# A feed-forward stage whose first two chunks are turned back by VectorE and transfers, with six up chunks first

## The chip, the cores and the metric

The kernel runs on one core of one Trainium2 chip. The metric is the device time of one execution in microseconds (us). In the profile's rows PE is TensorE (matrix products), PEld its weight loads, DVE is VectorE, ACT is ScalarE, POOL is GpSimd and SP is SyncE, whose queue issues most transfers.

## The reference

One decoder layer on a sequence of 256 positions and 1024 channels, in float32: a mixer of two branches (an mLSTM and block attention), a residual layer norm, then a gated MLP with a causal convolution and a second residual layer norm. The change touches only the MLP:

```python
def conv_gated_mlp(x, w_up, conv_ffn, w_down):
    u = causal_dwconv(jnp.einsum("bsd,df->bsf", x, w_up), conv_ffn)   # 3 taps over positions
    g, up = jnp.split(u, 2, axis=-1)                                  # 2816 channels each
    return jnp.einsum("bsf,fd->bsd", jax.nn.silu(g) * up, w_down)
# x = layer_norm(ALPHA * x + ffn, ln2_g, ln2_b)
```

## The kernel before

All weights are cut into chunks of 128 x 2048 numbers, which are worked off in one list (`chunk_order`, L45). One turn of the loop in `run` (L338) is one step: it puts out the elementwise work that the step before left behind, the splitting of the weights that are needed two steps later, the load of the chunk five steps ahead (`load`, three buffers), and then the step's matrix products. The order of the instructions on each engine is the order in which the program writes them; nothing is rearranged afterwards. Three buffers hold split weights and three banks (`ps_main`) hold results of chunks.

Every float32 product is made of three products of rounded parts. A tile is split by `split_into` (L92): ACT casts it to a high part, DVE subtracts that from the original and leaves the low part. `mm3` (L143) multiplies high by high, high by low and low by high.

The MLP has 22 up chunks and 11 down chunks. Up chunk i makes 128 gate channels and 128 value channels. `mm_feat` gives them with channels on partitions and positions along the free dimension: 16 accumulations of three matrix products, 48 in all. `up_evac` (L1095) then returns two pieces of elementwise work. `conv` scales by the last tap on ACT (L1107, two instructions) and adds the other two taps on DVE (L1111, four). `gate` applies Silu on ACT (L1118), multiplies on DVE (L1122), and splits the product into the hidden tile's high and low part `hh` (ACT, L94) and `hl` (DVE, L95); six buffers hold each. Down chunk d uses hidden tiles 2d and 2d + 1, first all products of the one, then all of the other, and accumulates into four banks (`step_dn`, L1131).

Up chunks 0 and 1 are different, because the first layer norm finishes the two halves of the positions one after the other. They are computed together with positions on partitions (`mm_tok`), first for the first 128 positions and then for the others. Their results have to be turned so that channels lie on partitions. In the kernel before, ACT copies the two results to `tu` (L1072), PE turns them by eight transposes of 128 x 128 between the two halves of up chunk 2 (`back`, L1074), and the elementwise work of chunks 0 and 1 is put out together with that of chunk 2, in the step of up chunk 3.

How elementwise work and weight splitting interleave is written out by hand: `elem_work` (L381) goes through a list in which `None` means "now one piece of the weights' splitting". `self.mixed[s]` may rewrite the list of step s. The attention part already turns tiles without PE: `turn` (L636) transposes 32 x 32 blocks on DVE and writes the result to memory in DRAM, and `turn_in` (L646) reads it back by four transfers in which the blocks have changed places; both transfers go through SP's queue.

Of the kernel before, what the change touches and what calls it, by code (L numbers as in the profile page):

```python
# [10 lines left out]
F32 = mybir.dt.float32  # L11
F32R = mybir.dt.float32r
# [6 lines left out]
P = 128  # L19
S = 256  # L20
# [4 lines left out]
NF = D_FF // P  # L25
# [19 lines left out]
def chunk_order():  # L45

    order = [("o", c) for c in range(4)]
    for g in range(NG):
        order += [("qm", g), ("qb", g), ("km", g), ("kb", g), ("vm", g), ("vb", g), ("ga", g), ("gb", g)]
    for c in (0, 2):  # L50
        order += [("wa", c), ("wa", c + 1), ("wb", c), ("wb", c + 1)]
    order += [("wo", c) for c in range(4)]
    order += [("up", i) for i in range(4)]
    for d in range(8):
        order += [("dn", d), ("up", 2 * d + 4), ("up", 2 * d + 5)]
    order += [("up", 20), ("up", 21), ("dn", 8), ("dn", 9), ("dn", 10)]
    assert sum(k == "up" for k, _ in order) == NF and sum(k == "dn" for k, _ in order) == NF // 2
    return order

# [13 lines left out]
class Kernel:  # L73
# [106 lines left out]
    def run(self):  # L180
# [4 lines left out]
        dram = ctx.enter_context(tc.tile_pool(name="dram", bufs=1, space=DRAM))  # L185
# [51 lines left out]
        for k, (s, c) in enumerate(cut):  # L237
            dma(xraw[:, k], self.xt_d[:, k])
            for t in (2, 3, s) if k < 2 else (2, s, 3):
                if t == s:  # L240
                    dma(raw[s][:, c], self.wst[s, :, c])
                elif k in pieces:
                    d = slice(k * 256, (k + pieces[k]) * 256)
# [13 lines left out]
        for k, (s, c) in enumerate(cut):  # L257
# [3 lines left out]
            n = pieces.get(k, 0)  # L261
            d = slice(k * 256, (k + n) * 256)
# [50 lines left out]
        for s, (kind, i) in enumerate(self.order):  # L313
            if kind == "qm":
# [3 lines left out]

        self.table = dram.tile([8, LTOE], F32, name="table")
        self.mrows = dram.tile([4, S], F32, name="mrows")  # L320
        self.flip = [[dram.tile([m, P, n * P], F32, name=f"flip{g}{i}")
                      for i, (m, n) in enumerate(((1, 3), (1, 3), (2, 2))[:3 if g < NG - 1 else 2])] for g in range(NG)]
        self.gates_schedule(bif)
# [14 lines left out]
        for s, (kind, i) in list(enumerate(self.order))[4:]:  # L338
# [25 lines left out]
            parts = [] if late else self.split_parts(s + 2)  # L364
# [268 lines left out]
        self.mixed[b + 2] = lambda w: w + [e1b, None, e1c, None, e1d, e1e]  # L633


    def turn(self, t, d):  # L636

        m, _, f = d.shape
        n, w = t.shape[1], t.shape[1] // m
        tmp = self.ap.tile([P, 4 * P], F32, tag="turn", name="turn", bufs=2)[:, 0:n * P]  # L640
        for k in range(m):
            self.nc.vector.transpose(tmp[:, k * f:(k + 1) * f].rearrange("p (b c i) -> p c b i", b=4, i=32),
                                     t[:, k * w:(k + 1) * w].rearrange("p c (b i) -> p c b i", b=4))
        self.nc.sync.dma_start(d.rearrange("m p f -> p m f"), tmp.rearrange("p (m f) -> p m f", m=m))
# [9 lines left out]
    def group_schedule(self, g):  # L654
# [212 lines left out]
        if g == 0:  # L867
            at(self.side_elem, 6, lambda: self.floor_exp())
        at(self.side_elem, 5 + o, turn(0))
        if last:  # L870
            self.mixed[b + 6] = lambda w: ([back(0), lambda: el_l(1), lambda: el_e(1), el_n1] + w
# [174 lines left out]
    def step_up(self, s, i, *a):  # L1046
        if i == 0:

            self.hid = {}
            self.pt_up = [self.ps_side([P, 2, S], f"ps_up{j}") for j in range(2)]  # L1050
        if i < 2:
            ks = list(range(i, KT)) + [0] * i
            for k in ks:
                if i == 0 and k == KT - 1:
                    self.x1_transpose(1, 0)
                for m in ((0, 1), (2,)) if (i, k) == (1, 1) else ((0, 1, 2),):
                    for j in range(2):
                        self.mm_tok(s - i + j, [self.pt_up[j][:, t, :] for t in range(2)], self.x1h, self.x1l,
                                    toks=(i,), ks=(k,), only=m, ends=(ks[0], ks[-1]))
            if i == 0:  # L1060
                def trans():
                    self.x1_transpose(1, 1)
                    for h in range(2):
                        self.x1_split(1, h)
                self.side_pe.setdefault(s, []).append(trans)
                return
            del self.w[s - 1], self.w[s]
            tu = self.fp.tile([P, 2, 2, S], F32, name="tu")

            def copy():  # L1070
                for j in range(2):
                    self.nc.scalar.copy(tu[:, j], self.pt_up[j])  # L1072

            def back():  # L1074
                for j in range(2):
                    ps = self.ps_side([P, 2, S], f"ps_upT{j}")
                    for f in range(2):
                        for t in range(2):
                            self.nc.tensor.transpose(ps[:, f, t * P:(t + 1) * P], tu[:, j, t, f * P:(f + 1) * P],
                                                     self.ident)  # L1080
                    self.pt_up[j] = ps
            self.evac[s] = copy
            self.back = back
            self.up_parts = [self.up_evac(j, lambda j=j: self.pt_up[j]) for j in range(2)]
            return
        ps = self.ps_main(f"ps_up{i}")
        self.mm_feat(s, ps, self.x1h, self.x1l, self.back if i == 2 else None)
        conv, gate = self.up_evac(i, lambda: ps)
        parts = [conv, None, None, gate]
        if i == 2:  # L1090
            (a0, b0), (a1, b1) = self.up_parts
            parts = [a0, a1, conv, b0, None, None, b1, gate]
        self.evac[s] = parts

    def up_evac(self, i, get_ps):  # L1095
        v, act, pp = self.nc.vector, self.nc.scalar, self.fp
        st = {}

        def tap(t, j):
            c = V_CFF + t * 2 * NF + j * NF + i  # L1100
            return self.vec[:, c:c + 1]

        def conv():
            ps = get_ps()
            cu = st["cu"] = pp.tile([P, 2, S], F32, tag="cu", name=f"cu{i}", bufs=3)
            for j in range(2):
                act.activation(cu[:, j, :], ps[:, j, :], AF.Copy, scale=tap(2, j))  # L1107
            for t in (1, 0):
                o = 2 - t
                for j in range(2):  # L1110
                    v.scalar_tensor_tensor(cu[:, j, o:], ps[:, j, :S - o], tap(t, j), cu[:, j, o:],  # L1111
                                           op0=ALU.mult, op1=ALU.add)

        def gate():
            cu = st["cu"]
            hh = pp.tile([P, S], F32R, tag="hh", name=f"hh{i}", bufs=6)
            hl = pp.tile([P, S], F32R, tag="hlo", name=f"hl{i}", bufs=6)
            act.activation(cu[:, 0, :], cu[:, 0, :], AF.Silu)  # L1118
            n = i - (NF - 3)
            if n >= 0:  # L1120
                self.row_sums(n)
            v.tensor_mul(cu[:, 0, :], cu[:, 0, :], cu[:, 1, :])  # L1122
            self.split_into(hh, hl, cu[:, 0, :])
            if n >= 0:
                self.split_sums(n)
            self.hid[i] = (hh, hl)
            if i == 5:
                self.load_ln_rows(1)
        return [conv, gate]

    def step_dn(self, s, d, *a):  # L1131
        nc = self.nc
        if d == 0:
            self.st = [self.ln_tiles(f"2_{t}") for t in range(2)]
            a0 = [self.ps_side([P, 512], f"ffn0{h}") for h in range(2)]
            a1 = [self.ps_side([P, 512], f"ffn1{h}") for h in range(2)]
            self.acc = [list(zip(a, ((0, 512), (512, 1024)))) for a in (a0, a1)]
            self.sums = self.fp.tile([P, 3, 2, 2], F32, name="sums")
            nc.gpsimd.memset(self.sums, 0.0)
            self.few = self.fp.tile([P, 8], F32, name="few")  # L1140
            self.unit = self.fp.tile([P, P], F32R, name="unit")
            self.res = [self.fp.tile([P, 256], F32R, name=f"res{n}") for n in "hl"]

            self.quarter = self.ps_side([P, 256], "ffn12")

        d0 = NF // 2 - 3

        def mm(dd, kk, t, ps, cols, fresh=0, more=False):
            b = self.col(self.order.index(("dn", dd)), kk * D)
            w = [x[:, b + cols[0]:b + cols[1]] for x in self.w[self.order.index(("dn", dd))]]  # L1150
            k = 2 * dd + kk
            hh, hl = (x[:, t * P:(t + 1) * P] for x in self.hid[k])
            self.mm3(ps, hh, hl, w[0], w[1], k == fresh and not more, k == (2 * d0 if t and not fresh else NF) - 1)

        def part(t, q):
            ps, cols = self.acc[t][q]
# [183 lines left out]
```

## Time and profile before

| | us |
|---|---|
| median of 3 runs (lowest to highest) | 478.37 (477.97 to 478.59) |
| the profiled execution | 478.42 |
| its span, first to last instruction | 476.6 |

| engine | busy us | share of the span | instructions |
|---|---|---|---|
| PE | 469.2 | 98% | 3788 |
| DVE | 368.3 | 77% | 644 |
| ACT | 309.9 | 65% | 540 |
| POOL | 36.6 | 8% | 74 |

Times in the rows are counted from the first instruction of the span. A row of a timeline gives the start, the duration, the engine, the line of the program, the operation, what is written from what, the shape, the count of instructions merged into the row, and in brackets the idle time before it with what ended it. Neighbouring instructions of one engine overlap a little, so the distance from start to start is less than the duration; the ends of PE's rows are modelled. The MLP begins at 287.6 us with up chunk 0; up chunk 2 begins at 299.69, the first down chunk at 311.61, and the last product starts at 470.22.

### The profile page before, as it was taken

How to read it: one execution, taken by the hardware profiler on the slowest of the kernel's cores; microseconds unless marked ns; L12 is line 12 of the kernel's file. 1: busy time of each engine (PE TensorE's matmuls, PEld its weight loads, DVE VectorE, ACT ScalarE, POOL GpSimd, SP SyncE). 2: the span in 40 equal slices, each digit the busy share in tenths (PEclk: the TensorE clock that was granted, in tenths of full speed). 3: DMA queues.
4: the chain of work that ended last, by engine and by line, in shares of the span. 5: the costliest groups of instructions: out<-in, count | busy, mean ns of one | idle time of the engine just before them, and what ended most of it. 6: DMA issues, size and time to landing. Idle time of an engine off the chain costs nothing.

```text
span 476.6 us, 9486 instructions
## 1 busy us (share of the span) xinstructions
PE 469.2 (98%) x3788; PEld 454.6 (95%) x3788; DVE 368.3 (77%) x644; ACT 309.9 (65%) x540; POOL 36.6 (8%) x74
## 2 busy tenths in 40 slices
PE   8999999999999999999999999999999999999994
PEld 6999999999999999999999999999999999999984
DVE  5886979787778778885685898879668666778876
ACT  5679878677868777977663634665555545656871
POOL 0315501000200020010100001000000000000000
PEclk9999999999999999999999999999999999999998
DMA  7895667934793477464957472736564545456202
GB/s 233 281 350 185 208 231 236 323 111 184 239 313 117 184 239 257 162 226 129 369 230 263 155 289 89 265 100 254 184 241 167 206 177 194 171 199 234 89 0 89
DMA packets 28958, 97.35 MB, mean 204 GB/s; under 512 B 10581, under 2 KB 15585, under 8 KB 19697
## 3 DMA queue, kind: packets, MB, share of 16 engines
q1 hardware_dynamic: 27682, 92.51, 55.5%
q0 software_dynamic: 1232, 4.24, 3.0%
q8 instruction: 29, 0.48, 0.4%
q14 instruction: 15, 0.12, 0.1%
HBM read 93.31 MB, written 3.42 MB: 203 GB/s over the span
## 4 chain that ended last, share of the span: by engine, by line
PE 98%; DVE 0%; ACT 0%; DVEq 0%; issue 0%; ACTq 0%
PE ps_up L148 25%; PE ffn L148 13%; PE ps_ga L148 5%; PE ps_kb L148 5%; PE ps_vm L148 5%; PE ps_vb L148 5%; PE mix L148 5%; PE ps_gb L148 5%; PE ps_wa L148 5%; PE ps_wb L148 5%; PE ps_qm L148 5%; PE ps_km L148 5%; PE ps_qb L148 5%; PE ps_o0a L427 1%; PE ps_o0b L427 1%; PE psn L148 1%
## 5 line engine op out<-in xcount | busy, mean ns | idle before, releaser
L95 DVE TENSOR_TENSOR wl<-raw,wh 128x1024 fp32r<-128x1024 f32 (+4 forms) x147 | 180.4, 1263 | 28.3 <-ACT wh L94 26.3
L94 ACT CAST wh<-raw 128x1024 fp32r<-128x1024 f32 (+4 forms) x147 | 151.8, 1077 | 10.6 <-DMA raw<-in_wst_dram 5.4
L148 PE MATMUL ps_up<-x1h,wl 128*128 128x256 f32 x320 | 88.5, 276 | 0.0
L148 PE MATMUL ps_up<-x1h,wh 128*128 128x256 f32 x320 | 88.4, 276 | 0.0
L148 PE MATMUL ps_up<-x1l,wh 128*128 128x256 f32 x320 | 88.4, 276 | 0.0
L148 PEld LDWEIGHTS ps_up<-x1l,wh 128*128 128x128 f32 x320 | 60.1, 188 | 0.4
L148 PEld LDWEIGHTS ps_up<-x1h,wh 128*128 128x128 f32 x320 | 60.1, 188 | 0.3
L148 PEld LDWEIGHTS ps_up<-x1h,wl 128*128 128x128 f32 x320 | 60.1, 188 | 0.0
L1111 DVE SCALAR_TENSOR_TENSOR cu<-ps_up,vec,cu 128x255 f32<-128x255 f32 (+1 forms) x80 | 33.0, 476 | 20.1 <-ACT cu L1107 20.1
L148 PE MATMUL ffn<-wh,hl 128*128 128x512 f32 (+2 forms) x94 | 35.5, 378 | 0.0
L148 PE MATMUL ffn<-wl,hh 128*128 128x512 f32 (+2 forms) x94 | 35.4, 377 | 0.0
L148 PE MATMUL ffn<-wh,hh 128*128 128x512 f32 (+2 forms) x94 | 35.3, 375 | 0.0
L94 ACT CAST hh<-cu 128x256 fp32r<-128x256 f32 x22 | 8.9, 406 | 40.4 <-DVE cu L1122 40.4
L1107 ACT ACTIVATE cu<-ps_up,vec 128x256 f32<-128x256 f32 x40 | 16.7, 469 | 22.1 <-PE ps_up L148 22.1
L148 PEld LDWEIGHTS ffn<-wh,hl 128*128 128x128 f32 x94 | 17.7, 188 | 3.2
L148 PEld LDWEIGHTS ffn<-wl,hh 128*128 128x128 f32 x94 | 17.7, 188 | 3.1
L148 PEld LDWEIGHTS ffn<-wh,hh 128*128 128x128 f32 x94 | 17.7, 188 | 3.1
L1009 POOL TENSOR_TENSOR rs<-rs,mhalf 128x1 f32<-128x1 f32 x3 | 2.1, 700 | 230.4 <-DVE rs L1008 230.4
L148 PE MATMUL ps_ga<-xth,wh 128*128 128x256 f32 x64 | 18.0, 281 | 0.0
L148 PE MATMUL mix<-wh,mgh 128*128 128x256 f32 x64 | 17.8, 279 | 0.0
L148 PE MATMUL ps_wa<-yah,wh 128*128 128x256 f32 x64 | 17.8, 277 | 0.0
L148 PE MATMUL ps_kb<-xth,wl 128*128 128x256 f32 x64 | 17.7, 277 | 0.0
(344 smaller groups left out, 1474.5 us busy)
## 6 DMA issues: line engine op xcount, KB each, us to landing
raw<-in_wst_dram SPq DMA_DIRECT2D x72, 1024.0 KB, 4.9
raw<-in_wst_dram SPq DMA_DIRECT2D x10, 512.0 KB, 6.5
raw<-in_wst_dram SPq DMA_DIRECT2D x8, 256.0 KB, 4.5
lnrow<-in_rows_dram POOLq DMA_DIRECT2D x4, 512.0 KB, 6.6
flip<-turn SPq DMA_DIRECT2D x8, 192.0 KB, 1.9
lg<-flip SPq DMA_DIRECT2D x32, 48.0 KB, 5.0
xraw<-in_xt_dram SPq DMA_DIRECT2D x8, 128.0 KB, 4.4
toe<-table POOLq DMA_DIRECT2D x4, 256.0 KB, 4.0
```

What stands on the lines that cost most here:

```text
L94: self.nc.scalar.copy(wh, raw)
L95: self.nc.vector.tensor_sub(wl, raw, wh.bitcast(F32))
L148: self.nc.tensor.matmul(ps, a[i], b[i], start=start and i == 0, stop=stop and i == 2)
L427: mm(ps[t], x[:, k, t * P:(t + 1) * P], w, start=start and k == 0, stop=stop and k == KT - 1)
L1009: nc.gpsimd.tensor_tensor(st["rs"], st["rs"], self.mhalf[:, 0:1], op=ALU.pow)
L1107: act.activation(cu[:, j, :], ps[:, j, :], AF.Copy, scale=tap(2, j))
L1111: v.scalar_tensor_tensor(cu[:, j, o:], ps[:, j, :S - o], tap(t, j), cu[:, j, o:], op0=ALU.mult, op1=ALU.add)
```

## The change

Three things change together.

The results of up chunks 0 and 1 are no longer turned by PE. After ACT's copies, DVE transposes them in 32 x 32 blocks into a new tile `tv` (two instructions of 128 x 512), SP writes them to memory in DRAM (two transfers of 256 KB), and one step later SP reads them back into `tu` (eight transfers of 64 KB). ACT then brings the blocks of each chunk into their natural order by two strided copies of 128 x 256 from `tu` to `tv` (`natural`). `conv` of chunks 0 and 1 reads `tv` in place of a PSUM bank.

The order of the chunks is new. Before: up 0 to 3, then a down chunk and two up chunks in turn (down 0, up 4, up 5, down 1, ...), at the end up 18 to 21 and down 8 to 10. Now: up 0 to 5, down 1, up 6, down 0, up 7, up 8, down 2, up 9, up 10, down 3, up 11, up 12, down 4, down 5, up 13 to 15, down 6, up 16, up 17, down 7, up 18 to 21, down 8 to 10. The accumulation therefore starts with hidden tile 2 (`fresh=2`).

The elementwise work of chunks 0 and 1 is spread over the steps of up 5 (copies and `conv` of chunk 0), down 1 (copies of chunk 1, `gate` of chunk 0) and up 6 (`conv` and `gate` of chunk 1). Their hidden tiles are allotted earlier, behind tile 3, so that the six buffers turn over in the order of use.

```diff
-    order += [("up", i) for i in range(4)]
-    for d in range(8):
-        order += [("dn", d), ("up", 2 * d + 4), ("up", 2 * d + 5)]
-    order += [("up", 20), ("up", 21), ("dn", 8), ("dn", 9), ("dn", 10)]
+    order += [("up", i) for i in range(6)]
+    for d, i in ((1, 6), (0, 7), (2, 9), (3, 11), (4, None), (5, 13), (6, 16), (7, 18), (8, None), (9, None), (10, None)):
+        n = {6: 1, 13: 3, 18: 4}.get(i, 2)
+        order += [("dn", d)] + ([] if i is None else [("up", i + j) for j in range(n)])
...
+        self.flip_up = [dram.tile([1, P, 4 * P], F32, name=f"flipu{j}") for j in range(2)]
...
-    def turn(self, t, d):
+    def turn(self, t, d, tmp=None):
...
+            tv = self.fp.tile([P, 2, 2, S], F32, name="tv")
+            rows = [tu[:, j].rearrange("p t (f d) -> p (t f) d", f=2) for j in range(2)]
+
             def copy():
                 for j in range(2):
                     self.nc.scalar.copy(tu[:, j], self.pt_up[j])
+                for j in range(2):
+                    self.turn(rows[j], self.flip_up[j], tv[:, j].rearrange("p f s -> p (f s)"))
 
             def back():
                 for j in range(2):
-                    ps = self.ps_side([P, 2, S], f"ps_upT{j}")
-                    for f in range(2):
-                        for t in range(2):
-                            self.nc.tensor.transpose(ps[:, f, t * P:(t + 1) * P], tu[:, j, t, f * P:(f + 1) * P],
-                                                     self.ident)
-                    self.pt_up[j] = ps
+                    self.turn_in(rows[j], self.flip_up[j])
+
+            def natural(j):
+                src = tu[:, j].rearrange("p t s -> p (t s)").rearrange("p (a t f i) -> p f t a i", a=4, t=2, f=2)
+                for f in range(2):
+                    self.nc.scalar.copy(tv[:, j, f].rearrange("p (t a i) -> p t a i", t=2, a=4), src[:, f])
+
             self.evac[s] = copy
-            self.back = back
-            self.up_parts = [self.up_evac(j, lambda j=j: self.pt_up[j]) for j in range(2)]
+            (a0, b0), (a1, b1) = [self.up_evac(j, lambda j=j: tv[:, j]) for j in range(2)]
+            self.mixed[s + 2] = lambda w: [back] + w
+            self.mixed[s + 3] = lambda w: w + [lambda: self.hid_tiles(0), lambda: self.hid_tiles(1)]
+            self.mixed[s + 4] = lambda w: [lambda: natural(0), w[0], a0, None, None, w[-1]]
+            self.mixed[s + 5] = lambda w: [lambda: natural(1), w[0], b0, None, None, w[-1]]
+            self.mixed[s + 6] = lambda w: [a1, None, None, b1] + w
             return
         ps = self.ps_main(f"ps_up{i}")
-        self.mm_feat(s, ps, self.x1h, self.x1l, self.back if i == 2 else None)
+        self.mm_feat(s, ps, self.x1h, self.x1l)
         conv, gate = self.up_evac(i, lambda: ps)
-        parts = [conv, None, None, gate]
-        if i == 2:
-            (a0, b0), (a1, b1) = self.up_parts
-            parts = [a0, a1, conv, b0, None, None, b1, gate]
-        self.evac[s] = parts
+        self.evac[s] = [conv, None, None, gate]
+
+    def hid_tiles(self, i):
+        self.hid[i] = tuple(self.fp.tile([P, S], F32R, tag=t, name=f"{n}{i}", bufs=6)
+                            for t, n in (("hh", "hh"), ("hlo", "hl")))
...
-        if d == 0:
+        if d == 1:
...
-        def mm(dd, kk, t, ps, cols, fresh=0, more=False):
+        def mm(dd, kk, t, ps, cols, fresh=2, more=False):
```

In the diff s is the step of up chunk 1, so s + 2 is that of up 3, s + 4 of up 5, s + 5 of down 1 and s + 6 of up 6.

More of the change, by code (lines that the diff above doesn't have):

```diff
@@ L633, in gates_schedule @@
         self.mixed[b + 2] = lambda w: w + [e1b, None, e1c, None, e1d, e1e]
-    def turn(self, t, d):
+    def turn(self, t, d, tmp=None):
         m, _, f = d.shape
         n, w = t.shape[1], t.shape[1] // m
-        tmp = self.ap.tile([P, 4 * P], F32, tag="turn", name="turn", bufs=2)[:, 0:n * P]
+        if tmp is None:
+            tmp = self.ap.tile([P, 4 * P], F32, tag="turn", name="turn", bufs=2)[:, 0:n * P]
         for k in range(m):
@@ L1115, in gate @@
             cu = st["cu"]
-            hh = pp.tile([P, S], F32R, tag="hh", name=f"hh{i}", bufs=6)
-            hl = pp.tile([P, S], F32R, tag="hlo", name=f"hl{i}", bufs=6)
+            if i not in self.hid:
+                self.hid_tiles(i)
+            hh, hl = self.hid[i]
             act.activation(cu[:, 0, :], cu[:, 0, :], AF.Silu)
@@ L1125, in gate @@
                 self.split_sums(n)
-            self.hid[i] = (hh, hl)
             if i == 5:
@@ L1152, in mm @@
             hh, hl = (x[:, t * P:(t + 1) * P] for x in self.hid[k])
-            self.mm3(ps, hh, hl, w[0], w[1], k == fresh and not more, k == (2 * d0 if t and not fresh else NF) - 1)
+            self.mm3(ps, hh, hl, w[0], w[1], k == fresh and not more, k == (2 * d0 if t and fresh == 2 else NF) - 1)
         def part(t, q):
```

## The prediction

> **What bounds the kernel now.** I read the chain of waits first (which engine carries the end), then the view of what PE waits for.
>
> ```profile
> PE 98%; DVE 0%; ACT 0%; DVEq 0%; issue 0%; ACTq 0%
> ```
>
> ```profile
> PE warm_ps L202 <- DVE warm L199: 1.3, 1, 1.3
> ```
>
> TensorE (PE) carries nearly the whole span, so a microsecond taken from it is one gained, and any other engine counts only where it makes PE wait. The second view has this one entry, 1.3 us at the very start: in the feed-forward stage PE never waits. So I need two clocks: PE's pace per chunk, and how far the evacuation on ScalarE (ACT) and VectorE (DVE) runs behind it. The pace is in PE's timeline around the first chunks (start, duration, engine, line, operation).
>
> ```profile
> 299.69 0.28 PE L148 MATMUL ps_up<-x1h,wh 128*128 128x256 f32 x1
> ...
> 302.41 0.28 PE L148 MATMUL ps_up<-x1h,wl 128*128 128x256 f32 x1
> 302.53 1.03 PE L1079 MATMUL ps_upT<-ident,tu 128*128 128x128 f32 x8
> ...
> 303.89 0.28 PE L148 MATMUL ps_up<-x1l,wh 128*128 128x256 f32 x1
> ...
> 311.61 0.39 PE L148 MATMUL ffn<-wh,hh 128*128 128x512 f32 x1
> ...
> 314.37 0.39 PE L148 MATMUL ffn<-wh,hh 128*128 128x512 f32 x1
> ...
> 317.10 0.28 PE L148 MATMUL ps_up<-x1h,wh 128*128 128x256 f32 x1
> ...
> 327.99 0.39 PE L148 MATMUL ffn<-wh,hh 128*128 128x512 f32 x1
> ```
>
> Between 317.10 and 327.99 stand two up chunks, 96 matmuls: 5.445 us a chunk, 113.4 ns a matmul. A down chunk takes 317.10 - 311.61 = 5.49 us; its second half, which needs the second of its two hidden tiles, begins 314.37 - 311.61 = 2.76 us in. The first half of up chunk 2 is slower: 24 matmuls from 299.69 to 302.53, 118 ns each, against 113.4 later.
>
> Now the evacuation, in one undisturbed up chunk: the ACT rows, then the DVE rows.
>
> ```profile
> 339.12 0.84 ACT L1107 ACTIVATE cu<-ps_up,vec 128x256 f32<-128x256 f32 x2 [3.06 <-PE ps_up L148]
> 339.85 1.90 ACT L94 CAST wh<-raw 128x2048 fp32r<-128x2048 f32 x1
> ...
> 344.44 0.41 ACT L94 CAST hh<-cu 128x256 fp32r<-128x256 f32 x1 [2.38 <-DVE cu L1122]
> 344.75 0.83 ACT L1107 ACTIVATE cu<-ps_up,vec 128x256 f32<-128x256 f32 x2
> ```
>
> ```profile
> 339.99 1.65 DVE L1111 SCALAR_TENSOR_TENSOR cu<-ps_up,vec,cu 128x255 f32<-128x255 f32 x4 [2.49 <-ACT cu L1107]
> 341.78 2.29 DVE L95 TENSOR_TENSOR wl<-raw,wh 128x2048 fp32r<-128x2048 f32 x1
> 343.99 0.42 DVE L1122 TENSOR_TENSOR cu<-cu 128x256 f32<-128x256 f32 x1
> ```
>
> One round: ACT scales (next ACT instruction 0.73 later), DVE adds the taps from 0.87 after ACT's start, then the weights' subtraction (2.21 to the next DVE instruction), the product, 0.45 later ACT's cast of the hidden tile, 0.31 later the next round. From 339.12 to 344.75 that is 5.63 us, more than PE's 5.445. Neither engine is full, but the round is one chain: the cast stands in ACT's queue behind the product, which stands in DVE's behind the weights. Up chunks in a row therefore make the evacuation late; a down chunk, with only weights to split, lets it catch up. That is the reading on which the forecast rests.
>
> **The parts.** First, the eight transposes on PE go. Matmul 302.41, the eight, and four matmuls up to 303.89 take 1.48 us; five plain matmuls would take 5 x 0.1134 = 0.57. Removed: 0.91 us. A few matmuls at the border of the half chunk probably stay slow: 0.02. **Gain 0.9 us**, fully on the path.
>
> ```profile
> L1079 PE MATMUL ps_upT<-ident,tu x8: 271/272/273, 302.5 to 303.3; 128*128 128x128 f32 x8
> ```
>
> The Trainium skill ("TensorE: Matmul & The Clock Gate", Part 4, PE-mode transpose) gives about 275 ns for one transpose in a kernel; the duration above agrees. An estimate by that figure frees 8 x 0.275 = 2.2 us, and the whole sum below would be 478.8. The timeline row rules it out, since the eight overlap and take 1.03 us together, so it gets no chance; the sum goes by the 0.91.
>
> Second, two DVE transposes of 128x512 and the transfers.
>
> ```profile
> L642 DVE STREAM_TRANSPOSE turn<-lg x8: 578/578/579, 68.9 to 212.2; 128x384 f32<-128x384 f32 x8
> L642 DVE STREAM_TRANSPOSE turn<-yt x6: 396/416/436, 78.8 to 173.6; 128x256 f32<-128x256 f32 x6
> 300.50 2.01 ACT L94 CAST wh<-raw 128x1024 fp32r<-128x1024 f32 x2
> 301.59 2.36 DVE L95 TENSOR_TENSOR wl<-raw,wh 128x1024 fp32r<-128x1024 f32 x2 [1.15 <-ACT wh L94]
> ```
>
> From 256 to 384 elements a transpose grows by 0.16 us, so 512 takes about 0.74 (bounds: 0.58, and 0.83 for twice the 256 one). The second can start when ACT's second copy ends at 300.6 (ACT's next cast starts at 300.50, overlapping by 0.1) and ends at 301.4, inside the 1.15 us in which DVE waits for ACT's cast anyway: nothing. Without that cover it would be 1.5 us in a step with 2 us to spare.
>
> ```profile
> L652 SPq DMA_DIRECT2D lg<-flip x32: 318/430/1101, 72.7 to 217.5; - x32
> L644 SPq DMA_DIRECT2D flip<-turn x11: 326/338/583, 69.6 to 212.8; - x11
> DMA to landing us min/median/max: 1.8/4.2/6.5
> ```
>
> SP issues 2 writes and 8 reads more, 2 x 0.34 + 8 x 0.43 = 4.1 us of its queue. The writes stand ahead of the load of up 6, which waits for the split of up 4 (DVE until 303.95) in any case. The reads wait for the writes, land at the latest around 304 + 4 + 6.5 = 314.5, and are first used at 316.5 (below); behind them stands the load of down 0, which waits for DVE's split of up 5 until 310. The half megabyte each way meets weights that are needed two steps later. Cost nothing; if a read came 1 us late, the evacuation, and so the pause below, would be 1 us later.
>
> Third, four copies on ACT ("natural"), 128x256, with 32-element runs. Nothing in the trace is exactly this.
>
> ```profile
> L531 ACT COPY vbf<-ps_vb x4: 373/373/374, 66.5 to 211.1; 128x256 f32<-128x256 f32 x4
> L94 ACT CAST pth<-lg x8: 402/417/427, 99.9 to 222.7; 128x256 fp32r<-128x256 f32 x8
> L775 ACT ACTIVATE yah<-yt,vec x6: 507/517/524, 101.0 to 187.0; 128x256 fp32r<-128x256 f32 x6
> ```
>
> The nearest is the cast of a turned tile, 417 ns; neighbours overlap by 0.1 (two scalings of 0.47 take 0.73), so 0.33 each, with 0.27 and 0.42 as ends.
>
> Fourth, the order. PE's clock afterwards: up 2 ends at 302.53 + 24 x 0.1134 + 0.02 = 305.27, up 3 at 310.72, up 4 at 316.16, up 5 at 321.61, down 1 at 327.10, up 6 at 332.54. Down 0 starts there, and at **335.30** asks for hidden tile 1. When is that ready? The rest of the durations come from the present first rounds (ACT, then DVE).
>
> ```profile
> 306.36 0.84 ACT L1107 ACTIVATE cu<-ps_up,vec 128x256 f32<-128x256 f32 x2 [1.62 <-PE ps_up L148]
> 307.21 1.28 ACT L1118 ACT_TABLE_LOAD   x1
> 309.73 2.00 ACT L94 CAST wh<-raw 128x1024 fp32r<-128x1024 f32 x2
> ```
>
> ```profile
> 304.04 3.21 DVE L1111 SCALAR_TENSOR_TENSOR cu<-ps_upT,vec,cu 128x255 f32<-128x255 f32 x8
> 307.23 1.65 DVE L1111 SCALAR_TENSOR_TENSOR cu<-ps_up,vec,cu 128x255 f32<-128x255 f32 x4
> ...
> 310.81 2.36 DVE L95 TENSOR_TENSOR wl<-raw,wh 128x1024 fp32r<-128x1024 f32 x2 [0.53 <-ACT wh L94]
> 313.09 0.42 DVE L1122 TENSOR_TENSOR cu<-cu 128x256 f32<-128x256 f32 x1
> 313.98 0.43 DVE L95 TENSOR_TENSOR hl<-cu,hh 128x256 fp32r<-128x256 f32 x1 [0.47 <-ACT hh L94]
> ```
>
> Four taps take 1.6 us (eight from 304.04 to 307.23), two half splits 2.28 (310.81 to 313.09), the first beginning 1.08 after ACT's cast starts. ACT takes up a finished chunk 0.19 after PE has begun the next (306.36; PE's next, counted back from 311.61, began at 306.17). Today tile 1 is complete at 314.41, and its low half is asked for two matmuls (2 x 5.49/24) after 314.37, at 314.83: already close.
>
> - Step up 3: ACT scales from 305.46; DVE taps 306.33, split of up 5 from 307.93, product 310.21 (the table load ends earlier, at 309.4), cast 310.66, ACT free 310.97.
> - Step up 4: scaling 310.97, taps 311.84, split of down 1 313.44, product 315.72, cast 316.17, ACT free 316.48.
> - Step up 5: two natural copies to 317.14, scaling of up 4 to 317.87, of up 0 to 318.60. DVE: taps 318.01 to 319.61 and to 321.21, split of up 6 to 323.42, product, cast 323.87, ACT free 324.18.
> - Step down 1: two natural copies to 324.84, scaling of up 5 from there; taps 325.71 to 327.31, product of up 0, cast 327.76, ACT free 328.07 and only then the casts for down 0; DVE's split 329.15 to 331.43, product of up 5, cast 331.88, ACT free 332.19.
> - Step up 6: scaling of up 1 332.19, taps 333.06; cast for up 7 from 332.92; its split when that cast ends, 1.93 later, 334.85 to 337.06; product of up 1, cast 337.51 to **337.92**.
>
> PE stands from 335.30 to about 337.95: **2.65 us**. The excess is the naturals (1.32), a second round of taps in step up 5 (1.6) and the 0.2 that each round exceeds PE's; step down 1, which could have caught up, holds the gate of up 0 and a late up 5. With naturals at 0.27 the pause is 2.4, at 0.42 it is 3.0. Behind PE's waiting matmul stand the rest of down 0 and everything after it; who waits for PE there is the evacuation of up 7, which uses the pause to catch up. All later chunks are only shifted: the weight splits are early (up 7 at 337, needed at 340.9), hidden tiles 2 to 15 are ready at least a chunk ahead of their use, the down chunks 4 and 5 side by side only need splits, and from up 16 on the order is the old one.
>
> Sum against the profiled execution's own 478.42 us (the median of the three is 478.37): 478.42 - 0.9 + 2.6 = **480.1**.
>
> **The rivals.** (1) No pause: the evacuation keeps up, and hidden tile 1's cast ends by 335.3. Then only the transposes count: 478.42 - 0.9 = 477.5. It decides from 1.7 us of pause downwards (below that slower turns into no measurable change), and needs 2.6 us out of the chain. For it: naturals could slip into ACT's idle 2.38 us before a cast. Against: instructions of an engine start in order in every row above, and the second pair is issued behind that cast.
>
> (2) The slow pace does not end. Now 118 ns a matmul end at the transposes; without that break the second half of up 2 and chunks 3 to 5 could run at 118: 24 + 144 = 168 matmuls x 4.8 ns = 0.8 us. Down 0 would come 0.8 later, but the evacuation only 0.3, so the pause shrinks by 0.5: 480.4. For it: the slow pace crosses the border from up 1 to up 2. Against: in the rest of the stage 113.4 holds without transposes.
>
> (3) The pause costs clock as well. Windows of the span's end: time, PE busy, PE weight load, DVE, ACT, POOL, clock, DMA.
>
> ```profile
> 470.00:471.00 1.00, 0.50 (x5) 0.29 (x3) 0.02 (x1) 0.41 (x2) 0.18 (x1) 1.00 0.00 0
> 473.00:474.00 1.00, 0.00 (x0) 0.00 (x0) 0.32 (x1) 0.00 (x0) 0.00 (x0) 0.79 0.72 264
> 474.00:475.00 1.00, 0.00 (x0) 0.00 (x0) 0.00 (x0) 0.00 (x0) 0.00 (x0) 0.50 0.75 260
> ```
>
> PE ends at 470.5 and the granted clock falls to half at about 473.6, 3.1 us later. A pause of 2.6 stays just short. If the clock fell for as long again, 3.1 us at half pace cost 1.6: 481.7. The Trainium skill ("TensorE: Matmul & The Clock Gate", Part 1) names an idle window of about 3.4 us that runs freely; the 3.1 us here agrees within its phase, and by that rule 2.6 does not suffice.
>
> **How the numbers follow.** Forecast 480.1 with 0.60 (its own range 479.3 to 480.9, from naturals and 0.4 us of rounding in a chain of some thirty steps); rival 1 0.17, rival 2 0.17, rival 3 0.06. The range 478.6 to 481.3 takes in forecast and rival 2 and leaves out most of rivals 1 and 3. This kernel's three runs lie within 0.6 us, and about 0.2% (0.96 us) is what can be told from no change: slower means above 479.3, faster below 477.4. Slower: 0.60 x 0.93 + 0.17 x 0.95 + 0.06 = 0.78. Rival 1 lies at the edge, four parts in ten faster: 0.07. The same: 0.15.
>
> **What would show it.** PE's waits get one new entry, on the cast hh (or hl) of tile 1, of 2 to 3 us, in the middle of the second down chunk; ACT's second naturals stand behind a cast; 0.8 us less PE work; DVE's new transposes end before the split. Wrong if down 0 runs in 5.49 us without a gap, if a wait stands on a flip transfer or a weight split instead, or if the 118 ns pace goes on past up 2.

## The result, and the profile after

The changed kernel takes 481.39 us (median of six runs, 479.79 to 481.82) against 478.27 for the kernel before (477.92 to 478.59, on the same chip). The ratio is 1.0058, with a 95% interval of 1.0045 to 1.0071: slower by 2.8 us (the medians differ by 3.1). The forecast was 480.1; the median stands 1.3 above it and 0.1 above the upper end of the range. Counted by the ratio from the 478.42 with which the prediction began, the result is 481.2, 0.1 inside the range: it lies at its very edge. The profiled execution took 481.64 us, with a span of 479.9.

First the chain of waits and the view of what PE waits for, as before.

```profile
PE 88%; DVE 4%; DMA 3%; ACT 2%; issue 1%; SPq 0%; DVEq 0%; ACTq 0%
```

```profile
PE ffn L148 <- ACT hh L94: 2.3, 1, 2.3
PE warm_ps L202 <- DVE warm L199: 1.3, 1, 1.3
```

The chain now leaves PE for a tenth of the span, because it is followed back from the new wait into the evacuation and its weights. The second view shows the cause in one row: a wait of PE in the feed-forward stage, where there had been none, once, 2.3 us, for ACT's cast of a hidden tile. PE's timeline at that place (start, duration, engine, line, operation, and in brackets the idle time with what ended it):

```profile
335.26 0.39 PE L148 MATMUL ffn<-wl,hh 128*128 128x512 f32 x1
335.49 0.39 PE L148 MATMUL ffn<-wh,hl 128*128 128x512 f32 x1
338.19 0.79 PE L148 MATMUL ffn<-wh,hh 128*128 128x512 f32 x1 [2.31 <-ACT hh L94]
338.78 0.63 PE L148 MATMUL ffn<-wl,hh 128*128 128x512 f32 x1
339.21 0.63 PE L148 MATMUL ffn<-wh,hl 128*128 128x512 f32 x1
...
341.59 0.39 PE L148 MATMUL ffn<-wh,hl 128*128 128x512 f32 x1
...
342.51 0.28 PE L148 MATMUL ps_up<-x1h,wh 128*128 128x256 f32 x1
```

The pause is where the prediction put it, in the middle of the second down chunk (down 0), between its twelfth and thirteenth matmul. At the pace of the rows before, the thirteenth would have started at 335.72; it started at 338.19. PE stood for 2.47 us. What comes next was not in the forecast: the following matmuls last 0.63 instead of 0.39 us and start 0.43 apart instead of 0.23, until about 341.3. (PE's busy time therefore rises, from 469.2 to 470.4 us, although eight transposes are gone.) The windows of the same place say why (time, then the busy time of PE, weight load, DVE, ACT and POOL, the granted clock, the DMA share and GB/s).

```profile
336.00:337.00 1.00, 0.00 (x0) 0.00 (x0) 1.00 (x1) 0.00 (x0) 0.00 (x0) 1.00 0.00 0
337.00:338.00 1.00, 0.00 (x0) 0.00 (x0) 0.70 (x2) 0.27 (x1) 0.00 (x0) 0.97 0.00 0
338.00:339.00 1.00, 0.81 (x2) 0.71 (x3) 0.51 (x2) 1.00 (x4) 0.00 (x0) 0.50 0.95 131
...
341.00:342.00 1.00, 1.00 (x5) 0.82 (x4) 1.00 (x1) 0.00 (x0) 0.00 (x0) 0.82 0.40 164
342.00:343.00 1.00, 1.00 (x8) 0.87 (x8) 1.00 (x2) 0.00 (x0) 0.00 (x0) 1.00 0.00 0
```

The granted clock is full up to 337.94 (0.97 over the window from 337 to 338) and half from there on; the 0.82 of the window from 341 to 342 puts its return at about 341.36. So it is half for 3.4 us, beginning 0.25 us before PE starts again. Down 0 lasts from 332.96 to 342.51, 9.55 us instead of 5.49: 4.06 more, of which 2.47 are the pause and 1.6 the slow matmuls. That gives 478.3 - 0.9 + 2.5 + 1.6 = 481.5.

ACT's timeline shows how the cast came to be late.

```profile
316.51 0.41 ACT L94 CAST hh<-cu 128x256 fp32r<-128x256 f32 x1 [2.12 <-DVE cu L1135]
316.83 0.71 ACT L1088 COPY tv<-tu 128x256 f32<-128x256 f32 x2
317.44 0.83 ACT L1119 ACTIVATE cu<-ps_up,vec 128x256 f32<-128x256 f32 x2
318.17 0.90 ACT L1119 ACTIVATE cu<-tv,vec 128x256 f32<-128x256 f32 x2
318.97 1.90 ACT L94 CAST wh<-raw 128x2048 fp32r<-128x2048 f32 x1
...
324.10 0.41 ACT L94 CAST hh<-cu 128x256 fp32r<-128x256 f32 x1 [2.92 <-DVE cu L1135]
324.41 0.71 ACT L1088 COPY tv<-tu 128x256 f32<-128x256 f32 x2
...
337.73 0.40 ACT L94 CAST hh<-cu 128x256 fp32r<-128x256 f32 x1 [2.38 <-DVE cu L1135]
```

The rounds run as forecast: both pairs of natural copies stand behind a cast that waits for DVE, ACT's idle time before these casts (2.12, 2.92) is not used by them, and the last cast ends at 338.13, against the 337.92 of the prediction.

### The profile page after: what moved, and what is told of

Read it like the earlier page. It is cut to its first block, busy times and chain, and to the rows that moved or that the text cites. A ratio compares the mean times of both kernels' runs of the same rounds, so it can differ in the third digit from the quotient of the medians.

```text
span 479.9 us, 9494 instructions
## 1 busy us (share of the span) xinstructions
PE 470.4 (98%) x3780; PEld 455.0 (95%) x3780; DVE 368.3 (77%) x646; ACT 311.0 (65%) x544; POOL 37.6 (8%) x74
## 4 chain that ended last, share of the span: by engine, by line
PE 88%; DVE 4%; DMA 3%; ACT 2%; issue 1%; SPq 0%; DVEq 0%; ACTq 0%
PE ps_up L148 18%; PE ffn L148 11%; PE ps_ga L148 5%; PE ps_kb L148 5%; PE mix L148 5%; PE ps_vm L148 5%; PE ps_vb L148 5%; PE ps_gb L148 5%; PE ps_wa L148 5%; PE ps_wb L148 5%; PE ps_qm L148 5%; PE ps_km L148 5%; PE ps_qb L148 5%; DMA raw<-in_wst_dram 3%; DVE wl L95 2%; PE ps_o0a L428 1%
```

## The experiments

The first run has no edit. Each of the next five is one edit of the changed kernel, the seventh an edit of the kernel before. The diffs are shortened: the `lambda` of the list entries is left out. Ratios are always to the kernel before, run on the same chip. Five of the seven profiles (all but those of down 0 later and of the natural copies earlier) have one more wait of PE, 0.4 to 1.1 us for a weight cast at about 7 us, far ahead of the change; of the views of waits only the rows of the MLP are shown.

### The changed kernel once more

No edit. Was the half clock an accident of one execution?

> The changed kernel once more, for the share of its runs in which the clock falls. Theory (pause plus clock): every run has the pause of about 2.45 us on hidden tile 1 in the second down chunk; where the mean granted clock of a run is 0.994 or 0.995 the clock also fell to half for one stretch of 3.41 us, and that run takes about 481.4 us; a run with 0.997 or 0.998 takes about 479.8. Most runs fall. Rival (the clock follows something else in the new order): clock and time do not go together.

Measured: 481.3 us (480.91 to 481.57, five runs), ratio 1.0065 (1.0053 to 1.0077). The profiled execution has the pause at the same place (2.31 us) and the half clock again, but later:

```profile
336.00:338.00 2.00, 0.10 (x1) 0.10 (x1) 1.53 (x3) 0.56 (x2) 0.00 (x0) 1.00 0.00 0
338.00:340.00 2.00, 2.00 (x8) 1.51 (x9) 1.68 (x5) 2.00 (x3) 0.00 (x0) 0.83 0.96 262
340.00:342.00 2.00, 2.00 (x6) 1.53 (x5) 1.86 (x2) 0.69 (x2) 0.00 (x0) 0.50 0.62 262
```

Here the clock falls at 339.3, 1.4 us after PE has started again at 337.90, and so the slow stretch lies partly in the up chunk behind. The loss is no accident of the profiled execution. My expectation that the mean clock of an execution would tell executions with the fall from those without was wrong: means of 0.992 to 0.999 go with times within 0.7 us. The mean also holds the half clock behind PE's work, at the end of the span, and that stretch differs: 2.0 us in the profile of the result, 3.9 here. One thing the mean does say. A stretch of 3.41 us at half takes 0.0036 off it, so the execution with 0.999 (480.91 us) cannot have had one in the middle; why it is hardly shorter than the others is not shown.

### Down 0 one chunk later

```diff
-    for d, i in ((1, 6), (0, 7), (2, 9), ...
-        n = {6: 1, 13: 3, 18: 4}.get(i, 2)
+    for d, i in ((1, 6), (0, 8), (2, 9), ...
+        n = {8: 1, 13: 3, 18: 4}.get(i, 2)
```

> Down 0 is moved behind up 7 (before: behind up 6), nothing else changes. Theory: down 0 asks for hidden tile 1 5.45 us later, 2 to 3 us after it is ready, so there is no pause and no fall of the clock, and only the eight transposes that were taken out count: 477.4 us (478.3 - 0.9), ratio to the kernel before 0.998, PE's waits hold only the one entry at the start. Rival (evacuation too slow altogether, or transfers in the way): a wait moves to a later chunk and the time stays above 479.

Measured: 477.18 us (476.85 to 477.48, ten runs), ratio 0.9976 (0.9967 to 0.9985), faster than both kernels. First PE's waits, then ACT's row of the cast, then PE's of the matmul that needs it.

```profile
PE warm_ps L202 <- DVE warm L199: 1.3, 1, 1.3
```

```profile
337.54 0.41 ACT L94 CAST hh<-cu 128x256 fp32r<-128x256 f32 x1 [1.74 <-DVE cu L1135]
```

```profile
340.71 0.39 PE L148 MATMUL ffn<-wh,hh 128*128 128x512 f32 x1
```

The cast ends at 337.95, as late as in the changed kernel, but PE asks for it only at 340.71. With the pause gone, the half clock is gone too, and what is left is a gain of 1.1 us (0.7 to 1.6), which holds the 0.9 of the eight transposes. So the pause and what follows from it are the whole loss, as far as the interval tells, and the new path of chunks 0 and 1 over DVE and memory costs nothing that can be measured.

### The natural copies earlier

```diff
-    mixed[s + 3] = w + [hid_tiles(0), hid_tiles(1)]
-    mixed[s + 4] = [natural(0), w[0], a0, None, None, w[-1]]
-    mixed[s + 5] = [natural(1), w[0], b0, None, None, w[-1]]
+    mixed[s + 3] = w[:-1] + [natural(0), w[-1], hid_tiles(0), hid_tiles(1)]
+    mixed[s + 4] = [w[0], a0, None, None, natural(1), w[-1]]
+    mixed[s + 5] = [w[0], b0, None, None, w[-1]]
```

Each pair is put ahead of the cast behind which it stood, into ACT's idle time.

> Each pair of natural copies is put one place earlier, into the time in which ACT waits for DVE ahead of the cast of a hidden tile: chunk 0's in the step of up 4 ahead of the gate, chunk 1's in the step of up 5 ahead of the gate. Theory: both pairs (4 x 0.305 us) leave the chain, the pause shrinks by 1.2 to about 1.2 us. If the clock does not fall then: 478.3 - 0.9 + 1.2 = 478.6; if it falls: 480.2. Rival (the pause hangs on DVE's taps alone, the copies lie in its shadow): the pause stays 2.4.

Measured: 478.66 us (478.29 to 480.11, twelve runs, eleven of them up to 479.06), ratio 1.0014 (1.0005 to 1.0022). PE's waits, PE's timeline and the windows:

```profile
PE ffn L148 <- ACT hh L94: 1.1, 1, 1.1
```

```profile
335.16 0.39 PE L148 MATMUL ffn<-wh,hl 128*128 128x512 f32 x1
336.64 0.50 PE L148 MATMUL ffn<-wh,hh 128*128 128x512 f32 x1 [1.10 <-ACT hh L94]
```

```profile
336.00:338.00 2.00, 1.36 (x6) 1.06 (x7) 1.22 (x4) 1.81 (x4) 0.00 (x0) 1.00 0.47 115
338.00:340.00 2.00, 2.00 (x13) 1.69 (x12) 1.85 (x4) 1.44 (x2) 0.00 (x0) 1.00 0.97 410
```

The wait shrinks by 1.2 us, close to the 1.32 that the prediction gave the four copies, and the clock stays full. The thirteenth matmul was due 0.23 after 335.16 and started 1.25 late, 0.15 more than the bracket counts, because the bracket begins at the modelled end of the matmul before. Down 0 takes 6.92 us, 1.43 more than undisturbed: these 1.25 and some 0.2 for running up again. With the transposes' 0.9 that is +0.5; the medians differ by 0.5, the ratio says +0.7. (The one run at 480.11 is not explained; the kernel before has two above 479 among its 22.) The total falls by 2.6 us against the changed kernel although the wait falls by 1.2. The rest is the clock.

### The natural copies twice

```diff
-    mixed[s + 4] = [natural(0), w[0], a0, None, None, w[-1]]
-    mixed[s + 5] = [natural(1), w[0], b0, None, None, w[-1]]
+    mixed[s + 4] = [natural(0), natural(0), w[0], a0, None, None, w[-1]]
+    mixed[s + 5] = [natural(1), natural(1), w[0], b0, None, None, w[-1]]
```

> Each pair of natural copies is done twice, in its place. Theory: 4 x 0.305 us are added to the chain, the pause grows by 1.2 to about 3.7 us and the clock falls in every run: 478.3 - 0.9 + 3.7 + 1.5 = 482.6. Rival (copies in the shadow): pause and time as in the changed kernel, 481.4.

Measured: 482.97 us (482.53 to 484.36, five runs), ratio 1.0108 (1.0094 to 1.0122).

```profile
PE ffn L148 <- ACT hh L94: 3.5, 1, 3.5
```

```profile
340.00:342.00 2.00, 2.00 (x6) 1.61 (x5) 1.79 (x5) 2.00 (x3) 0.00 (x0) 0.50 0.82 340
```

Four more copies lengthen the wait by 1.2 us, as four fewer in that place had shortened it: the copies enter the pause in full, 0.3 us each. The clock is half again, and down 0 takes 10.83 us: 3.69 of pause (335.67 to 339.36) and 1.65 of slow matmuls, as in the changed kernel. A longer pause costs more by its own length; the fall costs the same.

### Only the second pair earlier

```diff
-    mixed[s + 4] = [natural(0), w[0], a0, None, None, w[-1]]
-    mixed[s + 5] = [natural(1), w[0], b0, None, None, w[-1]]
+    mixed[s + 4] = [natural(0), w[0], a0, None, None, natural(1), w[-1]]
+    mixed[s + 5] = [w[0], b0, None, None, w[-1]]
```

> Only the second pair of natural copies (chunk 1's) is put early, into the step of up 5 ahead of the gate; the first pair stays. Theory: the pause is half way between, 2.45 - 0.6 = 1.85 us. This tells where the clock starts to fall: with 1.2 us it stayed, with 2.45 it fell. If it stays: 478.1 - 0.9 + 1.85 = 479.1; if it falls in all runs: 480.6; runs of both kinds mean that the place of the pause in the clock's windows decides.

Measured: 479.58 us (479.05 to 480.82, eleven runs, nine of them up to 479.82), ratio 1.0024 (1.0015 to 1.0032).

```profile
PE ffn L148 <- ACT hh L94: 1.7, 1, 1.7
```

```profile
338.00:340.00 2.00, 2.00 (x11) 1.61 (x10) 1.86 (x5) 1.85 (x2) 0.00 (x0) 1.00 0.91 381
```

The clock stays full in the profiled execution, and the mean clocks of all eleven, 0.996 to 0.999, are those of the kernel before, so it seems to have fallen in none of them; the two runs at 480.10 and 480.82 must have another reason, which is not shown. Down 0 takes 7.55 us, 2.06 more than undisturbed: 478.3 - 0.9 + 2.06 = 479.5, which is the time measured. With waits of 1.1 and 1.7 us the pause is paid once; with 2.3 and 3.5 it is paid once more in clock.

### Chunk 0 without its taps

```diff
-            for t in (1, 0):
+            for t in (1, 0) if i else ():
```

This is in `conv`. It takes one round of four taps (1.6 us of DVE) out of the step of up 5, to see what a second round there contributes to the pause.

> The four DVE tap additions of up chunk 0 are left out (so chunk 0 has only its last tap and the output differs by that). Reading A (the prediction's list of what makes up the pause, with 1.6 us for these taps): the pause shrinks to about 0.9 us, 478.1. Reading B (the chain followed step by step: without the taps the split of up 6 waits for ACT's cast, which ends only 0.7 us before the taps did): it shrinks by 0.6 to about 1.85 us, and the time is that of the kernel with only the second pair early.

Measured: 480.68 us in twelve runs that fall into two groups, five from 479.07 to 479.68 and seven from 480.65 to 482.86; ratio 1.0048 (1.0032 to 1.0065). The profiled execution (479.33) belongs to the lower group, and its clock is full throughout down 0. First PE's waits, then DVE's split of up 6:

```profile
PE ffn L148 <- ACT hh L94: 1.8, 1, 1.8
```

```profile
320.56 2.29 DVE L95 TENSOR_TENSOR wl<-raw,wh 128x2048 fp32r<-128x2048 f32 x1 [0.94 <-ACT wh L94]
```

Without the 1.6 us of taps the pause is only 0.5 shorter. The bracket says where the other 1 us went: DVE, free early, waits 0.94 for ACT's weight cast. In the changed kernel the same split starts at 321.45; PE's rows lie 0.34 earlier in this run (down 0 starts at 332.62 against 332.96), so the split comes 0.55 earlier, and that is what the pause loses. In the step of up 5, ACT's row (two copies, four scalings, a cast of 1.9) is almost as long as DVE's, so taking work from DVE alone brings little. Seven of the twelve runs took 1 to 3 us more. Six of them (480.70 to 482.86) have mean granted clocks of 0.992 to 0.995, and means below 0.996 occur elsewhere only in the kernels whose profiles show the half clock; the seventh (480.65) and the lower group have 0.996 to 0.999. So after a pause of this length the clock probably falls in some executions and not in others, but I have no trace of one of the six, and the seventh stays open.

### The kernel before, without the transposes

```diff
-        self.mm_feat(s, ps, self.x1h, self.x1l, self.back if i == 2 else None)
+        self.mm_feat(s, ps, self.x1h, self.x1l)
```

> The kernel before without the eight transposes on PE and nothing in their place (the elementwise work of up chunks 0 and 1 reads the unturned banks, so the output differs). Theory: 0.9 us less, 477.2, ratio 0.998, no new wait of PE. Rival (the slow pace of 118 ns a matmul goes on without the break): up chunks 2 and 3 stay at 118, and only 0.6 us is gained. Rival (by 275 ns a transpose): 2.2 us less, 475.9.

Measured: 477.68 us (477.41 to 478.19, eleven runs) against 478.30, ratio 0.9984 (0.9975 to 0.9993). PE's timeline, up chunk 2's first matmul and the first down chunk:

```profile
299.48 0.28 PE L148 MATMUL ps_up<-x1h,wh 128*128 128x256 f32 x1
...
310.50 0.39 PE L148 MATMUL ffn<-wh,hh 128*128 128x512 f32 x1
...
313.03 0.39 PE L148 MATMUL ffn<-wh,hl 128*128 128x512 f32 x1
313.37 0.50 PE L148 MATMUL ffn<-wh,hh 128*128 128x512 f32 x1
...
316.22 0.28 PE L148 MATMUL ps_up<-x1h,wh 128*128 128x256 f32 x1
```

The gain is smaller than the 0.9 expected, and my expectation of no new wait was a miss: the down chunk takes 5.72 us instead of 5.49. Two steps of 0.34 instead of 0.23, from 313.03 to 313.37 and from there on, are PE meeting the evacuation of hidden tile 1, which had been close already. From the start of up 2 to that of the down chunk it takes 11.02 us (299.48 to 310.50), in the kernel before 11.92: the 0.9 came off, and 0.23 went back. In the old order the transposes were therefore worth about 0.67 us in the trace, and 0.62 by the medians.

## Why the prediction was right and where it was wrong

**The transposes: right.** The kernel with down 0 later has no pause and is 1.1 us faster than before (interval 0.7 to 1.6), which holds the 0.9, and in the kernel before without them up 2 and up 3 are 0.90 shorter.

**DVE's transposes and the transfers: right in cost, wrong in time.** The rows of the tiles involved in the changed kernel: DVE's transposes, the writes with their landing, the reads with theirs, the natural copies.

```profile
L644 DVE STREAM_TRANSPOSE tv<-tu x2: 665/682/700, 300.8 to 301.4; 128x512 f32<-128x512 f32 x2
```

```profile
L646 SPq DMA_DIRECT2D flipu<-tv x2: 326/326/327, 301.6 to 302.1; - x2
DMA to landing us min/median/max: 6.1/6.1/6.1
```

```profile
L654 SPq DMA_DIRECT2D tu<-flipu x8: 303/429/432, 307.5 to 311.7; - x8
L1088 ACT COPY tv<-tu x4: 401/402/402, 316.8 to 324.7; 128x256 f32<-128x256 f32 x4
DMA to landing us min/median/max: 2.4/4.3/4.6
```

A transpose took 0.68 us, below the 0.74 chosen. The writes took 6.1 us to land, near the worst row shown, so the reads could only be issued from 307.5 and the last landed at about 311.7 + 4.6 = 316.3, not by 314.5. The first natural copy, at 316.83, needs only the four reads of chunk 0, and it stood behind the cast of 316.51 in any case. Of these the last was issued at about 309.3 and landed by 313.9, 3 us ahead. Nobody waited.

**The pause: right in place, cause and size.** 2.65 us predicted, 2.47 measured, at hidden tile 1's cast in down 0. The round of 5.63 us against PE's 5.445, the copies behind a cast and the absence of a catching-up step all stand in the rows; of these only the copies were tested by themselves. The natural copies have 0.305 us from one start to the next (317.44 - 316.83 for two), where 0.33 was chosen; moving them out and doubling them each changed the wait by 1.2 us.

**What makes up the pause: one share wrong.** "A second round of taps in step up 5 (1.6)" is not a term of that size: without the round the wait fell by 0.5. The step-by-step chain had the right end, since in it both engines' rows run side by side; the list behind the sum took one engine's row alone for the whole delay. The copies (1.2) and this round (0.5) leave about 0.6 of the wait of 2.31 to rounds that are longer than PE's chunk; that share was not taken out by itself.

**The slow pace (rival 2): did not happen.** In the changed kernel 118 ns a matmul end without any transpose:

```profile
302.95 0.28 PE L148 MATMUL ps_up<-x1h,wh 128*128 128x256 f32 x1
303.42 0.28 PE L148 MATMUL ps_up<-x1l,wh 128*128 128x256 f32 x1
...
303.99 0.28 PE L148 MATMUL ps_up<-x1h,wh 128*128 128x256 f32 x1
```

From 302.95 to 303.42 are four matmuls at 118 ns, from 303.42 to 303.99 five at 114, and it stays so. The change comes four matmuls into the second half of up 2; in the kernel before without its transposes it also comes there, at 302.78.

**The clock: the step that failed.** "A pause of 2.6 stays just short" is wrong. It compared the pause with the 3.1 us between the last matmul and the fall of the clock at the end of the span. That is one reading of how long PE may stand before the clock falls, and not a bound that a shorter pause keeps: here 2.47 us were enough. At the ends of the nine profiled spans the same distance is anything from 2.0 to 5.0 us. The last section shows why: in the traces the clock changes only at moments that are 3.413 us apart, and how long PE stood within one such step goes with whether it fell. Rival 3 happened, with a chance of 0.06. Its price came out, 1.6 us expected and 1.6 measured in down 0, 481.7 expected and 481.4 measured, but partly by luck: it supposed a fall "for as long again" as the 3.1 us, and the stretch is 3.41 us, of which PE worked in all but 0.25. The forecast for a pause without the fall is probably seen in one of the six runs of the changed kernel, 479.79 (its mean clock of 0.998 leaves no room for the stretch), and, with the pause shortened, in the kernel with one pair earlier.

**The whole account:** 478.3 - 0.9 (transposes) + 2.5 (pause) + 1.5 (half clock) = 481.4. The 1.5 is what is left of the median when the other terms are taken off; the traces give 1.6.

## What to carry to other kernels

Where PE bounds the stage, a pause of PE can be priced twice: its own length, and what the clock does behind it; the second comes in one piece, here 1.6 us on top of 2.5. Before chunks are moved, follow the chain of the evacuation round by round against PE's pace: rounds that are each a little longer than PE's chunk should add up until a chunk with less evacuation lets them catch up (read from the rows here, not tested alone), and the same late result cost nothing when its consumer stood one chunk later. In such a chain the engines' rows run side by side, so the work of one of them is not the delay that it causes.

## What the runs showed of the hardware

The granted clock fell to half after waits of PE of 2.3 us (the changed kernel, both profiles; 2.47 from matmul to matmul) and 3.5, and stayed full in the profiles with waits of 1.1, 1.7 and 1.8. It was half for one stretch of 3.4 us each time, however long the pause: 337.94 to 341.36, 339.31 to 342.73 and 339.21 to 342.62. The fall can come while PE works again: in the second profile of the changed kernel 1.4 us after its restart.

The clock changes only at moments that lie a whole number of steps of 3.413 us apart, on a grid. In the profiles with a half stretch it returned at 341.36, 342.73 and 342.62, and it fell for the last time, behind PE's work, at 477.88, 475.84 and 479.16. Between lie 136.52, 133.11 and 136.54 us: 40, 39 and 40 times 3.413, which is also the length of the half stretch. The last falls are read from windows such as these, in this order: the changed kernel, the changed kernel once more, the natural copies earlier, only the second pair earlier, chunk 0 without its taps (the clock is the third number from the end).

```profile
477.00:478.00 1.00, 0.00 (x0) 0.00 (x0) 0.00 (x0) 0.00 (x0) 0.00 (x0) 0.94 0.98 352
```

```profile
475.00:476.00 1.00, 0.00 (x0) 0.00 (x0) 0.96 (x4) 0.00 (x0) 0.00 (x0) 0.92 0.00 0
```

```profile
474.00:475.00 1.00, 0.00 (x0) 0.00 (x0) 0.00 (x0) 0.00 (x0) 0.00 (x0) 0.92 0.98 357
```

```profile
476.00:477.00 1.00, 0.00 (x0) 0.00 (x0) 0.00 (x0) 0.00 (x0) 0.00 (x0) 0.72 0.00 0
```

```profile
475.00:476.00 1.00, 0.00 (x0) 0.00 (x0) 0.00 (x0) 0.00 (x0) 0.00 (x0) 0.78 0.95 341
```

Counted back from its last fall in steps of 3.413, the grid can be laid over the pause of every profile, also where the clock stayed full. The table has the time for which PE stood inside one step, from the modelled end of its last matmul. "End" is the stretch behind PE's last product.

| kernel | step of the grid | PE stood in it, us | clock after it |
|---|---|---|---|
| natural copies earlier | 334.90 to 338.31 | 1.09 | full |
| only the second pair earlier (0.57 more in the next step) | 333.07 to 336.49 | 1.16 | full |
| only the second pair earlier, end | 469.61 to 473.02 | 1.55 | full |
| chunk 0 without its taps | 335.61 to 339.02 | 1.71 | full |
| changed kernel once more, end | 472.43 to 475.84 | 1.95 | half |
| changed kernel once more | 335.90 to 339.31 | 2.00 | half |
| changed kernel | 334.53 to 337.94 | 2.06 | half |
| natural copies twice | 335.80 to 339.21 | 3.38 | half |

In these traces the border lies between 1.71 and 1.95 us inside one step, 50% to 57% of it. If that holds, the place of a pause matters: one that is cut in two by the grid, as with only the second pair earlier, counts less. That would explain why executions of the same kernel differ, as they do without chunk 0's taps. But the executions that differed were not traced, and no experiment moved one pause against the grid.

The Trainium skill ("TensorE: Matmul & The Clock Gate", Part 1) has the clock fall after an idle window of about 3.4 us. The length of the steps agrees with such a window, 3.413 us. That the window must be idle throughout does not: in the table 1.95 to 2.06 us of it were enough three times; only with the natural copies twice was nearly the whole window idle.

A wait costs somewhat more than the view of waits says, even where the clock stays: down 0 was longer than undisturbed by 1.43 us with a wait of 1.10, and by 2.06 with one of 1.73. About half of the 0.33 is the modelled end of the last matmul before it; of the rest most is the first step after it (0.34 us instead of 0.23).
